# Output projection of a mixer on one core: three chunks swept and five resident, the resident ones loaded directly, scaling shared, LayerNorm in two fused passes, VectorE's order fixed token tile by token tile

## The chip, the cores and the metric

The kernel runs on one core of a Trainium2 chip. The core has five engines with their own instruction queues: TensorE (PE, with PEld for its weight loads), VectorE (DVE), ScalarE (ACT), GpSimd (POOL) and SyncE (SP), which here issues nearly all DMAs. The engines wait for each other through semaphores. The metric is the device time of one execution in microseconds (us), the median of several runs. The programs are built by a scheduler that puts the instructions of each engine into one fixed order, so what stands behind a waiting instruction on its engine waits with it.

## The reference, cut to what matters

One post-norm layer on 512 tokens of width 1024, in float32. The change touches the end of the first sub-layer and the beginning of the second, and a helper that the last projection shares.

```
def _token_mixer(...):
    ...
    merged = gates[:, :, 0] * y_a + gates[:, :, 1] * y_b + gates[:, :, 2] * y_c
    return merged @ w_o
...
def _conv_ffn(h, w_up, conv_w, conv_b, w_down):
    z = h @ w_up                      # 1024 -> 5632
    ...                               # causal convolution of width 3
    return (jax.nn.silu(gate) * val) @ w_down   # 2816 -> 1024
...
x = LayerNorm(ALPHA * x + gate_t * _token_mixer(...)) * gain + bias
h = LayerNorm(x) * (1 + scale_f) + shift_f
x = LayerNorm(ALPHA * x + gate_f * _conv_ffn(h, ...)) * gain + bias
```

`gate_t`, `scale_f` and the like are rows that depend on the condition `c` only.

## The kernel before, in words

Every float32 matrix product is made of three products of rounded parts: an operand `w` is split into a high part `wh` and a remainder `wl`, and `mm3` (L103 to L106) issues wl·xh, wh·xl, wh·xh into one accumulator. The splitting costs ScalarE a copy (high part) and VectorE a subtraction (low part).

Tokens come in four tiles of 128 (t = 0 to 3), widths in halves of 512 (n = 0, 1). Weights come in chunks of 128 rows.

**The merge and the projection.** `merge(2, m, ...)` makes eight tiles `mg` with GpSimd (L374) and splits them into `mgh` and `mgl` (L986, L987). `project_out` (L1018) then multiplies by the eight chunks of `wo`, into eight accumulators `pyo` (one for each t and n). A chunk is loaded and scaled by the gate row `gttb` on GpSimd, both halves (`scaled_chunk`, L998 to L1016, the multiplication at L1003), and split. The first two chunks are swept: `o`, `oh`, `ol` are 1024 wide and live in rings of two, and each chunk goes through all eight accumulators. The other six are resident: their split parts (`o2h`, `o2l` and so on) have buffers of their own, so that the program can run token tile by token tile. All raw chunks come through one ring of three buffers with the tag `raw` (L82), which the early chunks of the next weight share. The same function makes the down projection at the end, with 22 chunks (`d`, 18 swept and 4 resident).

**Behind each token tile.** `chain(t, acc)` is `after_mixer`. It does, for two halves each: `residual` (VectorE: x1 = ALPHA·xr + pyo, L1079, and statistics, L1082), `ln_finish` (VectorE aggregates, L129; GpSimd computes 1/sqrt(var), a multiply-add L120, a power L123 and a product L132), `affine` (ScalarE, L1086), `gain_bias` (half 0 on GpSimd, half 1 on VectorE, multiplication L1092 and addition L1093), `second_stats` (VectorE, L1106, and `ln_finish` again), `second_norm` (ScalarE writes `xr`, L1113). When two token tiles are done, `second_modulation(tp, jp)` transposes them on TensorE (`pth`, L1125), and ScalarE and VectorE write `h2T0h`, `h2T0l` to `h2T7h`, `h2T7l` (L1133 to L1145).

**The up projection.** Six early pieces of `wup` (m = 0 to 5, split in `early_split` and `early_low`, L1049 to L1067) are multiplied with the first two token tiles as soon as `h2T` has them (`pzu`, 256 columns, `up_early`), later with the other two; the remaining 38 pieces run with all 512 columns.

**The gate row.** `gt_t = ada_rows(0, 0, "gtt")` (L809) sums up a row: ScalarE splits, GpSimd subtracts (`adal`, L734), four `pgt` products on TensorE (L739), and VectorE adds a bias. It stands between the first merge and the pooling products (`pmx`).

The order comes from a scheduler, save for a few places pinned with `issue_after`: `behind_split` puts condition rows behind a weight split, and `after(...)` with `marks` holds some of the second token pair's work behind `second_modulation`.

Of the kernel before, what the change touches and what calls it, by code (L numbers as in the profile page):

```python
# [50 lines left out]
def trunk(ctx: ExitStack, tc: tile.TileContext, A, out):  # L51
# [73 lines left out]
    last = []  # L125

    def ln_finish(st):
        mv = sm.tile([P, 2], F32, name="mv", tag="mv")
        a = nc.vector.bn_aggr(out=mv, in_=st.rearrange("p a b -> p (a b)"))  # L129
# [2 lines left out]
        b = nc.gpsimd.tensor_scalar(  # L132
            out=rs[:, 1:2], in0=mv[:, 0:1], scalar1=rs[:, 0:1], scalar2=-1.0, op0=ALU.mult, op1=ALU.mult
        )
# [864 lines left out]
    def scaled_chunk(src, gt, name, dst=None):  # L999
        raw = load(src, D, name)  # L1000
        for n in range(2):
            c = slice(n * 512, (n + 1) * 512)
            nc.gpsimd.tensor_tensor(out=raw[:, c], in0=raw[:, c], in1=gt[n], op=ALU.mult)  # L1003
        if dst is None:
            hi = wp.tile([P, D], F32R, name=name + "h", tag="whi")
            lo = wp.tile([P, D], F32R, name=name + "l", tag="wlo")
            nc.scalar.copy(out=hi, in_=raw)  # L1007
            nc.vector.tensor_tensor(out=lo, in0=raw, in1=f(hi), op=ALU.subtract)  # L1008
            return [hi[:, :512], hi[:, 512:]], [lo[:, :512], lo[:, 512:]]
        his = [dst(f"{name}h{n}") for n in range(2)]  # L1010
        los = [dst(f"{name}l{n}") for n in range(2)]
        for n in range(2):
# [2 lines left out]
            nc.vector.tensor_tensor(out=los[n], in0=raw[:, c], in1=f(his[n]), op=ALU.subtract)
# [52 lines left out]

    def residual_in(t):
        xr[t] = [act_t(f"xr{t}{n}", F32) for n in range(2)]  # L1070
        for n in range(2):
# [3 lines left out]
        x1[t] = [m_t(f"x1_{t}{n}") for n in range(2)]
        st_o[t] = sm.tile([P, 2, 6], F32, name="sto", tag="sto")

    def residual(t, n):
        nc.vector.scalar_tensor_tensor(  # L1079
            out=x1[t][n], in0=xr[t][n], scalar=ALPHA, in1=py_o[t][n], op0=ALU.mult, op1=ALU.add  # L1080
        )
        nc.vector.bn_stats(out=st_o[t][:, n, :], in_=x1[t][n])  # L1082

    def affine(t):
        for n in range(2):
            nc.scalar.activation(  # L1086
                x1[t][n], x1[t][n], AF.Identity, bias=rs_o[t][:, 1:2], scale=rs_o[t][:, 0:1]
            )

    def gain_bias(t):  # L1090
        for n, eng in ((0, nc.gpsimd), (1, nc.vector)):
            eng.tensor_tensor(out=x1[t][n], in0=x1[t][n], in1=lntg[n], op=ALU.mult)  # L1092
            eng.tensor_tensor(out=x1[t][n], in0=x1[t][n], in1=lntb[n], op=ALU.add)  # L1093
# [320 lines left out]
```

## Time and profile before

| | us |
|---|---|
| time, median of three runs | 1004.75 (1003.79 to 1005.43) |
| the profiled execution, its own time | 1005.82 |
| its span in the profile | 1003.7 |
| TensorE busy | 965.4 (96%) |
| VectorE, ScalarE, GpSimd busy | 601.0, 386.6, 301.1 |

The granted TensorE clock was 0.987 over the span. The profiled execution took 1005.82, so 2.1 us lie outside its span, and it is 1.07 above the median of the three runs. TensorE is busy nearly everywhere, so the time is the sum of its matmuls and of the places where it waits; the views that show those places are the list of waits and the timeline.

### The profile page before, as it was taken

Reading aid. Unit: us, or ns where it says so; the run is one execution under the profiler, and the core shown is the slowest. Engines: PE = TensorE matmul, PEld = TensorE weight load, DVE = VectorE, ACT = ScalarE, POOL = GpSimd, SP = SyncE. Lnnn points to the kernel's source line nnn. Section 1 sums busy time; section 2 is a strip of 40 time slices with the busy share of each in tenths; the row PEclk is TensorE's granted clock in tenths of the full one; section 3 lists DMA queues with packets and bytes.
Section 4 is the critical chain, followed back from the end, with each engine's and each line's share of the span. In section 5 each row is a group of like instructions: output and inputs, shape, how many; then the busy total and the mean of one; then the engine's idle time right before and its main releaser. Section 6 shows DMA issues by size and latency. Waiting matters only on the chain.

```text
span 1003.7 us, 12194 instructions
## 1 busy us (share of the span) xinstructions
PE 965.4 (96%) x4530; PEld 801.5 (80%) x4530; DVE 601.0 (60%) x923; ACT 386.6 (39%) x656; POOL 301.1 (30%) x311
## 2 busy tenths in 40 slices
PE   4999999999999999999999997999999999999996
PEld 3888888878877888888888876998888888788885
DVE  6947655546666565666434477777656675532267
ACT  3555555442323322433232234554434444321221
POOL 3555110212350011200011755421111121566664
PEclk9999999999999999999999998999999999999998
DMA  9713111115444542363222263124333433342322
GB/s 336 267 39 93 48 51 51 57 63 189 148 131 148 191 136 97 105 220 126 75 93 89 92 225 118 42 84 128 125 121 110 126 126 106 91 140 89 101 84 84
DMA packets 45274, 119.18 MB, mean 119 GB/s; under 512 B 5280, under 2 KB 8736, under 8 KB 45216
## 3 DMA queue, kind: packets, MB, share of 16 engines
q1 hardware_dynamic: 44784, 118.25, 36.0%
q8 instruction: 35, 0.57, 0.2%
q10 hardware_dynamic: 432, 0.17, 0.1%
q14 instruction: 23, 0.19, 0.1%
HBM read 116.30 MB, written 2.10 MB: 118 GB/s over the span
## 4 chain that ended last, share of the span: by engine, by line
PE 77%; DVE 6%; DMA 6%; POOL 5%; issue 3%; ACT 2%; SPq 0%; DVEq 0%; POOLq 0%; ACTq 0%
PE pzu L104 7%; PE pzu L106 7%; PE pzu L105 7%; PE pg L105 4%; PE pg L104 4%; PE pg L106 4%; PE pyd L106 4%; PE pyd L105 4%; PE pyd L104 4%; PE py L104 3%; PE py L105 3%; PE py L106 3%; PE pu L105 3%; PE pu L106 3%; PE pu L104 3%
## 5 line engine op out<-in xcount | busy, mean ns | idle before, releaser
L1270 POOL TENSOR_TENSOR zc<-zc 128x512 f32<-128x512 f32 x22 | 32.7, 1484 | 179.1 <-ACT zc L1269 179.1
L1003 POOL TENSOR_TENSOR d<-d,gtfb 128x512 f32<-128x512 f32 x44 | 72.9, 1676 | 42.1 <-DMA d<-in_wdn 39.3
L374 POOL TENSOR_TENSOR mg<-mg,th 128x512 f32<-128x512 f32 x16 | 22.7, 1416 | 150.5 <-DVE th L371 150.5
L1255 DVE SCALAR_TENSOR_TENSOR zc<-pzu,cols,zc 128x511 f32<-128x511 f32 x44 | 32.8, 747 | 50.1 <-ACT zc L1252 49.9
L1252 ACT ACTIVATE zc<-pzu,cols 128x512 f32<-128x512 f32 x44 | 34.2, 779 | 71.2 <-PE pzu L106 71.2
L1008 DVE TENSOR_TENSOR dl<-d,dh 128x1024 fp32r<-128x1024 f32 x18 | 29.0, 1613 | 52.1 <-ACT dh L1007 52.1
L91 DVE TENSOR_TENSOR wgl<-wg,wgh 128x1024 fp32r<-128x1024 f32 x22 | 27.7, 1260 | 48.6 <-ACT wgh L90 47.4
L721 DVE SCALAR_TENSOR_TENSOR ada<-adar,cact,ada 128x512 f32<-128x512 f32 x56 | 54.6, 1015 | 0.1
L90 ACT CAST wbh<-wb 128x1024 fp32r<-128x1024 f32 x24 | 25.2, 1051 | 70.3 <-PE py L106 65.9
L91 DVE TENSOR_TENSOR wbl<-wb,wbh 128x1024 fp32r<-128x1024 f32 x24 | 38.3, 1595 | 18.4 <-ACT wbh L90 18.3
L91 DVE TENSOR_TENSOR wupl<-wup,wuph 128x1024 fp32r<-128x1024 f32 x38 | 46.9, 1234 | 0.0
L1007 ACT CAST dh<-d 128x1024 fp32r<-128x1024 f32 x18 | 18.9, 1050 | 60.7 <-PE pyd L106 60.6
L90 ACT CAST wuph<-wup 128x1024 fp32r<-128x1024 f32 x38 | 39.5, 1039 | 0.0
L91 DVE TENSOR_TENSOR wsgl<-wsg,wsgh 128x1024 fp32r<-128x1024 f32 x16 | 19.6, 1224 | 33.2 <-ACT wsgh L90 33.2
L354 ACT ACTIVATE th<-pg 128x512 f32<-128x512 f32 x22 | 13.1, 597 | 59.5 <-PE pg L106 59.5
L1259 DVE SCALAR_TENSOR_TENSOR zc<-pzu,cols,zc 128x510 f32<-128x510 f32 x44 | 32.7, 747 | 1.3
L90 ACT CAST wsgh<-wsg 128x1024 fp32r<-128x1024 f32 x16 | 16.8, 1050 | 42.8 <-PE pu L106 38.0
L1003 POOL TENSOR_TENSOR o<-o,gttb 128x512 f32<-128x512 f32 x16 | 26.4, 1677 | 19.6 <-DMA o<-in_wo 16.7
L254 DVE SCALAR_TENSOR_TENSOR acc<-ada,cact,acc 128x256 f32<-128x256 f32 x48 | 29.2, 671 | 0.0
L642 POOL TENSOR_SCALAR pe<-pe,mx 128x128 f32<-128x128 f32 (+3 forms) x32 | 16.8, 533 | 35.7 <-DVE mx L641 26.3
L90 ACT CAST wgh<-wg 128x1024 fp32r<-128x1024 f32 x22 | 23.1, 1051 | 10.1 <-PE pu L106 4.7
L776 POOL TENSOR_TENSOR asum<-apad 128x527 f32<-128x527 f32 x8 | 8.5, 1065 | 56.8 <-issue 25.8
(1375 smaller groups left out, 3182.9 us busy)
## 6 DMA issues: line engine op xcount, KB each, us to landing
wup<-in_wup SPq DMA_DIRECT2D x44, 512.0 KB, 3.5
adar<-in_ada SPq DMA_DIRECT2D x64, 256.0 KB, 3.9
wb<-in_wb SPq DMA_DIRECT2D x24, 512.0 KB, 3.5
wg<-in_wg SPq DMA_DIRECT2D x22, 512.0 KB, 3.6
d<-in_wdn SPq DMA_DIRECT2D x22, 512.0 KB, 3.5
ada<-in_ada SPq DMA_DIRECT2D x32, 256.0 KB, 5.0
wsg<-in_wsg SPq DMA_DIRECT2D x16, 512.0 KB, 3.6
wa<-in_wa SPq DMA_DIRECT2D x8, 512.0 KB, 3.6
```

Of the source, the lines that this page charges most:

```text
L90: nc.scalar.copy(out=hi[:, :n], in_=raw[:, :n])
L91: ins = nc.vector.tensor_tensor(out=lo[:, :n], in0=raw[:, :n], in1=f(hi[:, :n]), op=ALU.subtract)
L104: nc.tensor.matmul(o, wh, xl, start=start, stop=False)
L105: nc.tensor.matmul(o, wl, xh, start=False, stop=False)
L106: nc.tensor.matmul(o, wh, xh, start=False, stop=stop)
L254: ins = nc.vector.scalar_tensor_tensor(out=acc[i], in0=src, scalar=cact[:, k : k + 1], in1=acc[i], op0=ALU.mult, op1=ALU.add,)
L721: nc.vector.scalar_tensor_tensor(out=acc[n], in0=src, scalar=cact[:, k : k + 1], in1=acc[n], op0=ALU.mult, op1=ALU.add,)
L1003: nc.gpsimd.tensor_tensor(out=raw[:, c], in0=raw[:, c], in1=gt[n], op=ALU.mult)
L1252: nc.scalar.activation(t, pz, AF.Identity, bias=cols[:, cc + 3 : cc + 4], scale=cols[:, cc + 2 : cc + 3])
L1255: nc.vector.scalar_tensor_tensor(out=t[:, 1:512], in0=pz[:, 0:511], scalar=cols[:, cc + 1 : cc + 2], in1=t[:, 1:512], op0=ALU.mult, op1=AL ...
L1259: nc.vector.scalar_tensor_tensor(out=t[:, 2:512], in0=pz[:, 0:510], scalar=cols[:, cc : cc + 1], in1=t[:, 2:512], op0=ALU.mult, op1=ALU.add,)
L1270: nc.gpsimd.tensor_tensor(out=val, in0=val, in1=gate, op=ALU.mult)
```

## The change

Five things are done.

1. `ada_rows(0, 0, "gtt")` moves from behind the first merge to the middle of the gating mixer's v halves.
2. The projection has three swept chunks and five resident ones. A resident chunk, in this projection and in the down projection, is loaded as two halves straight into buffers of the `act` pool (`o3w`, `d18w` and so on), no longer through the ring `raw`.
3. In the mixer's projection half 0 of a chunk is scaled on GpSimd and half 1 on VectorE; in the down projection both stay on GpSimd.
4. The first LayerNorm is made of two fused VectorE passes: `centre`, (x − mean)·gain, and `scale_again`, x·rs + bias, with the statistics of the second norm behind it. ScalarE's `affine` and the multiplications and additions of `gain_bias` go. `x` is loaded before the projection into the buffers that held `mg`, and becomes x1 in place.
5. VectorE's order around the token tiles is fixed with `in_turn`: the splits of `wup` 1 to 4 first, then tile 0 complete, tile 1 complete, then tiles 2 and 3 with the modulations between.

```
-    gt_t = ada_rows(0, 0, "gtt")
...
     v0 = uv_half(2, "v", lambda q: behind_split(ada_piece, 1, q))
+    gt_t = ada_rows(0, 0, "gtt")
...
     def scaled_chunk(src, gt, name, dst=None):
-        raw = load(src, D, name)
-        for n in range(2):
-            c = slice(n * 512, (n + 1) * 512)
-            nc.gpsimd.tensor_tensor(out=raw[:, c], in0=raw[:, c], in1=gt[n], op=ALU.mult)
+        if dst is None:
+            raw = load(src, D, name)
+            parts = [raw[:, :512], raw[:, 512:]]
+        else:
+            his = [dst(f"{name}h{n}") for n in range(2)]
+            los = [dst(f"{name}l{n}") for n in range(2)]
+            parts = [act_t(f"{name}w{n}", F32) for n in range(2)]
+            for n in range(2):
+                nc.sync.dma_start(out=parts[n], in_=src[:, n * 512 : (n + 1) * 512])
+        for n, eng in ((0, nc.gpsimd), (1, nc.vector if name[0] == "o" else nc.gpsimd)):
+            eng.tensor_tensor(out=parts[n], in0=parts[n], in1=gt[n], op=ALU.mult)
...
+    def in_turn(work, *args):
+        with ExitStack() as order:
+            for ins in vector_order:
+                order.enter_context(tc.issue_after(ins))
+            vector_order[:] = [work(*args).ins]
...
+    def residual(t):
+        ...
+            nc.vector.scalar_tensor_tensor(
+                out=x1[t][n], in0=x1[t][n], scalar=ALPHA, in1=py_o[t][n], op0=ALU.mult, op1=ALU.add
+            )
+            nc.vector.bn_stats(out=st[:, n, :], in_=x1[t][n])
+        ...
+    def centre(t):
+        for n in range(2):
+            ins = nc.vector.scalar_tensor_tensor(
+                out=x1[t][n], in0=x1[t][n], scalar=mv_o[t][:, 0:1], in1=lntg[n],
+                op0=ALU.subtract, op1=ALU.mult,
+            )
+        return ins
+
+    def scale_again(t):
+        ...
+            nc.vector.scalar_tensor_tensor(
+                out=x1[t][n], in0=x1[t][n], scalar=rs_o[t][:, 0:1], in1=lntb[n],
+                op0=ALU.mult, op1=ALU.add,
+            )
+            nc.vector.bn_stats(out=st[:, n, :], in_=x1[t][n])
+        rs_o[t] = ln_finish(st)
...
-    def affine(t):
-        for n in range(2):
             nc.scalar.activation(
-                x1[t][n], x1[t][n], AF.Identity, bias=rs_o[t][:, 1:2], scale=rs_o[t][:, 0:1]
-            )
-
-    def gain_bias(t):
-        for n, eng in ((0, nc.gpsimd), (1, nc.vector)):
-            eng.tensor_tensor(out=x1[t][n], in0=x1[t][n], in1=lntg[n], op=ALU.mult)
-            eng.tensor_tensor(out=x1[t][n], in0=x1[t][n], in1=lntb[n], op=ALU.add)
...
     def after_mixer(t, py):
         py_o[t] = py
+        in_turn(residual, t)
         if t == 2:
+            in_turn(second_modulation, 0, 0)
+        in_turn(centre, t)
+        if t == 2:
+            in_turn(second_modulation, 0, 1)
+        in_turn(scale_again, t)
+        second_norm(t)
+        if t == 2:
+            in_turn(second_modulation, 0, 2)
+            in_turn(second_modulation, 0, 3)
+            early_split(5)
+            early_low(5, nc.gpsimd)
...
-    project_out(lambda k: A["wo"][k], KT, 6, mg_hi, mg_lo, gt_t, act_t, after_mixer, "o")
+    project_out(
+        lambda k: A["wo"][k], KT, 5, mg_hi, mg_lo, gt_t, act_t, after_mixer, "o", before_tokens
+    )
```

How the built order moves is seen at three places. The first is TensorE where token tile 0 gets its last products of the projection. `pyo_5095` and `pyo_5096` are the two halves of tile 0 before, `pyo_5097` and `pyo_5098` those of tile 1; these rows are the 104th to 114th of the projection's 192 matmuls. Before:

```order
L104 MATMUL pyo_5095<-o7l0_5233,mgh7_5067 128x512
L105 MATMUL pyo_5095<-o7h0_5231,mgl7_5068 128x512
L106 MATMUL pyo_5095<-o7h0_5231,mgh7_5067 128x512
L104 MATMUL pyo_5097<-o7l0_5233,mgh7_5067 128x512
L105 MATMUL pyo_5097<-o7h0_5231,mgl7_5068 128x512
L106 MATMUL pyo_5097<-o7h0_5231,mgh7_5067 128x512
L104 MATMUL pyo_5098<-o5l1_5210,mgh5_4999 128x512
L105 MATMUL pyo_5098<-o5h1_5208,mgl5_5000 128x512
L104 MATMUL pyo_5096<-o7l1_5234,mgh7_5067 128x512
L105 MATMUL pyo_5096<-o7h1_5232,mgl7_5068 128x512
L106 MATMUL pyo_5096<-o7h1_5232,mgh7_5067 128x512
```

Now tile 0 has `pyo_5121` and `pyo_5122`, tile 1 `pyo_5123` and `pyo_5124`, and `pyo_5128` is the last half of tile 3; the rows are the 166th to 177th of the 192:

```order
L104 MATMUL pyo_5128<-o6l1_5270,mgh6_5036 128x512
L104 MATMUL pyo_5121<-o7l0_5283,mgh7_5067 128x512
L105 MATMUL pyo_5121<-o7h0_5281,mgl7_5068 128x512
L106 MATMUL pyo_5121<-o7h0_5281,mgh7_5067 128x512
L104 MATMUL pyo_5122<-o7l1_5284,mgh7_5067 128x512
L105 MATMUL pyo_5122<-o7h1_5282,mgl7_5068 128x512
L106 MATMUL pyo_5122<-o7h1_5282,mgh7_5067 128x512
L104 MATMUL pyo_5123<-o7l0_5283,mgh7_5067 128x512
L105 MATMUL pyo_5123<-o7h0_5281,mgl7_5068 128x512
L106 MATMUL pyo_5123<-o7h0_5281,mgh7_5067 128x512
L104 MATMUL pyo_5124<-o7l1_5284,mgh7_5067 128x512
L105 MATMUL pyo_5124<-o7h1_5282,mgl7_5068 128x512
```

Tile 0's two halves were complete after matmul 106 and 114 of 192, and are now after 169 and 172; tile 1's moved from 109 and 121 to 175 and 178. TensorE now runs the resident chunks chunk by chunk.

The second place is VectorE behind the projection's last split. Before, the work of the first two token tiles (`x1_0`, `x1_1`) starts between splits of `wup`:

```order
L1065 TENSOR_TENSOR upl01_5280<-wup_5275,uph01_5278 128x512
L1015 TENSOR_TENSOR o7l1_5234<-o7_5227,o7h1_5232 128x512
L1079 SCALAR_TENSOR_TENSOR x1_00_5289<-xr00_5285,pyo_5095 128x512
L1082 BN_STATS sto_5291<-x1_00_5289 128x6
L1079 SCALAR_TENSOR_TENSOR x1_01_5290<-xr01_5286,pyo_5096 128x512
L1079 SCALAR_TENSOR_TENSOR x1_10_5306<-xr10_5302,pyo_5097 128x512
L1065 TENSOR_TENSOR wupl_5325<-wup_5322,wuph_5324 128x512
L1082 BN_STATS sto_5291<-x1_01_5290 128x6
```

Now the splits of `wup` 1 to 4 stand ahead, and behind them tile 0 as a whole (shown without buffer numbers of `pyo`, `mv` and `rs`; `x_00` and `x_01` are tile 0's halves):

```order
L1089 SCALAR_TENSOR_TENSOR x_00_5105<-x_00_5105,pyo 128x512
L1089 SCALAR_TENSOR_TENSOR x_01_5106<-x_01_5106,pyo 128x512
L1092 BN_STATS sto<-x_00_5105 128x6
L1092 BN_STATS sto<-x_01_5106 128x6
L1094 BN_AGGR mv<-sto 128x2
L1101 SCALAR_TENSOR_TENSOR x_00_5105<-x_00_5105,mv,lntg_5071 128x512
L1101 SCALAR_TENSOR_TENSOR x_01_5106<-x_01_5106,mv,lntg_5073 128x512
L1110 SCALAR_TENSOR_TENSOR x_00_5105<-x_00_5105,rs,lntb_5075 128x512
L1110 SCALAR_TENSOR_TENSOR x_01_5106<-x_01_5106,rs,lntb_5077 128x512
L1114 BN_STATS st<-x_00_5105 128x6
L1114 BN_STATS st<-x_01_5106 128x6
L129 BN_AGGR mv<-st 128x2
```

Tile 1's first instruction stood three places behind tile 0's first; it now follows the last of these twelve, and tile 1's own twelve come before anything of tile 2.

The third place is ScalarE in the down projection, where `dh` is the high part of a swept chunk (18 in all), and `d18h` to `d21h` those of the resident ones. Before, they come at the end, behind fifteen more swept chunks:

```order
L1007 CAST dh<-d 128x1024 x15
L1014 CAST d18h_8125<-d_8121 128x512
L1014 CAST d18h_8126<-d_8121 128x512
L1007 CAST dh<-d 128x1024
L1014 CAST d19h_8137<-d_8133 128x512
L1014 CAST d19h_8138<-d_8133 128x512
```

Now they stand between the fourth and the eighth swept chunk:

```order
L1017 CAST d18h_8115<-d18w_8119 128x512
L1012 CAST dh<-d 128x1024
L1017 CAST d18h_8116<-d18w_8120 128x512
L1017 CAST d19h_8129<-d19w_8133 128x512
L1017 CAST d19h_8130<-d19w_8134 128x512
L1012 CAST dh<-d 128x1024
L1017 CAST d20h_8143<-d20w_8147 128x512
L1017 CAST d20h_8144<-d20w_8148 128x512
L1017 CAST d21h_8157<-d21w_8161 128x512
L1012 CAST dh<-d 128x1024
```

GpSimd scales them in the same order, so a swept chunk's `dh` now waits behind resident ones on both engines.

More of the change, by code (lines that the diff above doesn't have):

```diff
@@ L1030, in project_out @@
         ws = {k: scaled_chunk(src(k), gt, f"{name}{k}", dst) for k in range(nk - resident, nk)}
+        if hook:
+            hook()
         for t in range(TT):
@@ new lines, in centre @@
+    def centre(t):
+        for n in range(2):
+            ins = nc.vector.scalar_tensor_tensor(
+                out=x1[t][n], in0=x1[t][n], scalar=mv_o[t][:, 0:1], in1=lntg[n],
+                op0=ALU.subtract, op1=ALU.mult,
+            )
+        return ins
+    def scale_again(t):
+        st = sm.tile([P, 2, 6], F32, name="st", tag="st")
+        for n in range(2):
+            nc.vector.scalar_tensor_tensor(
[4 more added lines that the diff above has]
+        rs_o[t] = ln_finish(st)
+        return aggregated[0]
@@ L1070, in residual_in, with second_norm @@
+    def second_norm(t):
         xr[t] = [act_t(f"xr{t}{n}", F32) for n in range(2)]
         for n in range(2):
-            nc.sync.dma_start(
-                out=xr[t][n], in_=A["x"][t * P : (t + 1) * P, n * 512 : (n + 1) * 512]
-            )
[L1075 to L1080, printed above, removed]
-        )
-        nc.vector.bn_stats(out=st_o[t][:, n, :], in_=x1[t][n])
@@ L1103, in second_stats @@
-    def second_stats(t):
-        st = sm.tile([P, 2, 6], F32, name="st", tag="st")
-        for n in (1, 0):
-            nc.vector.bn_stats(out=st[:, n, :], in_=x1[t][n])
-        rs = ln_finish(st)
-        marks[t] = list(last)
-        return rs
-    def second_norm(t, rs):
-        for n in range(2):
-            a = nc.scalar.activation(
-                xr[t][n], x1[t][n], AF.Identity, bias=rs[:, 1:2], scale=rs[:, 0:1]
-            )
-        marks[t].append(a.ins)
+            nc.scalar.activation(
+                xr[t][n], x1[t][n], AF.Identity, bias=rs_o[t][:, 1:2], scale=rs_o[t][:, 0:1]
+            )
@@ L1210, in trunk @@
+    early_split(0)
+    early_low(0, nc.vector)
+    for t in range(TT):
+        x1[t] = [m_t(f"x1_{t}{n}") for n in range(2)]
+        for n in range(2):
+            nc.sync.dma_start(
+                out=x1[t][n], in_=A["x"][t * P : (t + 1) * P, n * 512 : (n + 1) * 512]
+            )
+    project_out(
+        lambda k: A["wo"][k], KT, 5, mg_hi, mg_lo, gt_t, act_t, after_mixer, "o", before_tokens
+    )
     pzs = {}
@@ L1243, in trunk @@
             else:
-                with after(3) if m < NE + 2 else ExitStack():
-                    uh, ul = wsplit(A["wup"][m], D, "wup")
+                uh, ul = wsplit(A["wup"][m], D, "wup")
                 pz = ps("pzu")
```

118 lines of the change are left out of this document (33 added, 85 removed).

## The prediction, made before the changed kernel was run

> **What bounds the kernel now.** Read first is the page's line of busy times, then the list of TensorE's waits (engine, line waited for: us in total, times, longest), then TensorE's timeline (start, us, instruction, and in brackets the idle time before it and what ended it).
>
> ```profile
> PE 965.4 (96%) x4530; PEld 801.5 (80%) x4530; DVE 601.0 (60%) x923; ACT 386.6 (39%) x656; POOL 301.1 (30%) x311
> ...
> PE pth L1125 <- ACT xr L1113: 5.7, 2, 4.6
> ...
> PE pgt L739 <- POOL adal L734: 1.2, 2, 0.7
> PE pyd L104 <- DVE dl L1008: 1.0, 2, 0.8
> ...
> PE pyo L104 <- DVE o5l L1015: 0.7, 1, 0.7
> ```
>
> TensorE is busy 96% of the span, so a change pays only where TensorE waits. The waits near the change are these four: behind the projection (`pth`), at the gate row (`pgt`), in the projection (`pyo`), and a small one in the down projection (`pyd`).
>
> ```profile
> 569.46 0.40 PE L104 MATMUL pyo<-ol,mgh 128*128 128x512 f32 x1
> ...
> 588.77 0.50 PE L104 MATMUL pyo<-o5l,mgh 128*128 128x512 f32 x1 [0.65 <-DVE o5l L1015]
> ...
> 615.66 0.39 PE L106 MATMUL pyo<-o7h,mgh 128*128 128x512 f32 x1
> 620.60 1.39 PE L1125 MATMUL pth<-ident,xr 128*128 128x128 f32 x4 [4.56 <-ACT xr L1113]
> 623.10 2.82 PE L1125 MATMUL pth<-ident,xr 128*128 128x128 f32 x12 [1.11 <-ACT xr L1113]
> 625.58 0.58 PE L104 MATMUL pzu<-h2T0l,uph 128*128 128x256 f32 x1
> ...
> 631.05 0.39 PE L104 MATMUL pzu<-h2T2l,uph 128*128 128x256 f32 x1 [0.83 <-DVE h2T2l L1145]
> ...
> 664.78 0.28 PE L106 MATMUL pzu<-h2T7h,uph 128*128 128x256 f32 x1
> 664.90 0.63 PE L104 MATMUL pzu<-h2T0l,wuph 128*128 128x512 f32 x2
> ```
>
> I call E the start of the projection's last matmul, 615.66. The up projection starts at E + 9.9, and its first matmul with all 512 columns, behind which nothing of this stage is late any more, at E + 49.2. Everything that the change does to LayerNorm must show in that second number. The windows (length, busy time and count of PE, PEld, DVE, ACT, POOL, then the granted clock) show the clock in the halt, and the pace of undisturbed matmuls (here PE alone):
>
> ```profile
> 616.00:620.50 4.50, 0.04 (x1) 0.00 (x0) 4.47 (x9) 0.76 (x2) 3.59 (x6) 0.81 0.00 0
> 620.50:629.00 8.50, 7.27 (x32) 6.43 (x33) 4.69 (x8) 7.23 (x14) 5.41 (x11) 0.50 0.00 0
> ...
> 873.60:995.20 121.60, 121.42 (x528) 1.00 0.31 100
> ```
>
> 528 matmuls of 512 columns in 121.6 are 0.230 each; one of 256 columns takes 0.12 (664.78 to 664.90).
>
> **The gate row: −1.8.**
>
> ```profile
> 300.24 0.40 PE L106 MATMUL py<-o7h,wbh 128*128 128x512 f32 x1
> 301.37 0.50 PE L739 MATMUL pgt<-adal,onesr 128*128 128x512 f32 x1 [0.73 <-POOL adal L734]
> ...
> 303.18 0.39 PE L104 MATMUL pmx<-po0l,wpoolh 128*128 128x512 f32 x1
> ```
>
> From 300.24 to 303.18 five steps take 2.94, where five steps of 0.230 are 1.15: 1.8 are waits for GpSimd's `adal`. In its new place the row was summed long before, and the four `pgt` stand amid gating matmuls. It could gain nothing, if `pmx` then waits for the pooling sums, and not more than 1.8; I take 1.8, as no `pmx` wait stands in the list.
>
> **The projection itself: −2.3.** Its 191 steps last 615.66 − 569.46 = 46.2, and at 0.230 they would last 43.9. The 2.3 are waits for low parts from `o5l` on (the list holds the two largest). GpSimd explains them:
>
> ```profile
> L1003 POOL TENSOR_TENSOR o<-o,gttb 128x512 f32<-128x512 f32 x16 | 26.4, 1677 | 19.6 <-DMA o<-in_wo 16.7 <-DVE mgl L987 2.9
> ```
>
> It scaled 16 halves at 1.677, and stood idle 16.7 for their loads, since all chunks pass a ring of three. Now five chunks have buffers of their own, and GpSimd scales half as much. TensorE also needs them later: chunk 3 after 72 matmuls (16.6), each next one 5.5 further. Bounds: 2.3 gained, or, if `o3` and `o4` are each as late as `o5` was, 2.3 gained and as much lost again. I take the gain. VectorE gets eight multiplications more, hidden behind the 5.5 per chunk.
>
> **LayerNorm: +4.7.** This is the term that decides. Tile 0 was complete 78 matmuls ahead of the end (114 of 192), so most of two LayerNorms lay beside the projection. Now it is complete after matmul 169 and 172: the 169th starts 23 × 0.230 = 5.3 ahead of E and ends 0.39 later, so VectorE can begin at E − 4.9. What it then does in a row is priced by these (in the second piece: line, names, count | busy, mean ns):
>
> ```profile
> 607.82 0.69 DVE L1082 BATCH_NORM_STATS2 sto<-x 128x6 f32<-128x512 f32 x1
> 608.42 0.67 DVE L1079 SCALAR_TENSOR_TENSOR x<-xr,pyo 128x512 f32<-128x512 f32 x1
> 609.01 0.20 DVE L129 BATCH_NORM_AGGREGATE mv<-sto 128x2 f32<-128x12 f32 x1
> ```
>
> ```profile
> L1295 DVE SCALAR_TENSOR_TENSOR out<-out,mv,lnfg 128x512 f32<-128x512 f32 x8 | 5.7, 749 | 0.1
> ```
>
> Starts lie 0.60 apart for a statistic or a residual, 0.08 less than its duration; the fused form, which the last LayerNorm already uses, takes 0.749, so a pace of 0.67. A tile is 2 residuals and 4 statistics at 0.60, 4 fused passes at 0.67, 2 aggregations at 0.2: 6.7, and some 0.3 where an instruction needs the one ahead of it: 7.0. Two tiles, one behind the other, end at E + 9.1. The power between the two passes lies beside `centre` (two passes, 1.4) but for the 0.2 within that 0.3:
>
> ```profile
> 606.54 0.20 DVE L129 BATCH_NORM_AGGREGATE mv<-sto 128x2 f32<-128x12 f32 x1
> ...
> 606.85 0.51 POOL L120 TENSOR_SCALAR pw<-mv 128x1 f32<-128x1 f32 x1 [6.30 <-DVE mv L129]
> 607.44 0.88 POOL L123 TENSOR_TENSOR rs<-pw,neghalf 128x1 f32<-128x1 f32 x1
> 608.42 0.27 POOL L132 TENSOR_SCALAR rs<-mv,rs 128x1 f32<-128x1 f32 x1
> ...
> 608.72 1.52 ACT L1086 ACTIVATE x<-x,rs 128x512 f32<-128x512 f32 x2 [1.75 <-POOL rs L132]
> ```
>
> From the aggregate's end to ScalarE are 2.0 here, and 1.8 where the power isn't slowed; I take 1.8: `xr` of tile 1 starts at E + 10.9.
>
> ```profile
> 622.24 1.52 ACT L1113 ACTIVATE xr<-x,rs 128x512 f32<-128x512 f32 x2 [0.98 <-POOL rs L132]
> ...
> 625.09 0.43 DVE L1145 TENSOR_TENSOR h2T0l<-h2f,h2T0h 128x256 fp32r<-128x256 f32 x1 [3.25 <-ACT h2T0h L1142]
> 625.55 0.54 DVE L1137 TENSOR_SCALAR h2T1h<-pth,scfc,shfc 128x256 fp32r<-128x256 f32 x1
> 626.12 0.42 DVE L1145 TENSOR_TENSOR h2T1l<-h2f,h2T1h 128x256 fp32r<-128x256 f32 x1
> ```
>
> From there to the first `pzu` were 3.3 (622.24 to 625.58), so the up projection starts at E + 14.2, 4.3 later than before.
>
> Then the second token pair is late. VectorE reaches `h2T0l` at 10.9 + 2.85 = E + 13.75. It still owes tile 2's fused passes and second statistics (4.3), four pairs of modulation writes (1.3 each by the last three rows: 5.2) and all of tile 3 (7.0): E + 30.3. `upl5` on GpSimd now falls beside tile 3's `centre`, which has a price:
>
> ```profile
> 615.81 1.17 DVE L1092 TENSOR_TENSOR x<-x,lntg 128x512 f32<-128x512 f32 x1 [1.00 <-ACT x L1086]
> ...
> 617.62 0.68 DVE L1079 SCALAR_TENSOR_TENSOR x<-xr,pyo 128x512 f32<-128x512 f32 x1
> ```
>
> ```profile
> 617.11 1.72 POOL L1093 TENSOR_TENSOR x<-x,lntb 128x512 f32<-128x512 f32 x1
> ```
>
> Beside a GpSimd operation the one with both inputs in SBUF took 1.17 instead of 0.68, while the residual, which reads an accumulator, kept 0.68. One such slowing is 0.5: E + 30.8, and with 1.8 and 3.3 the second half can start at E + 35.9. TensorE is done with the first half at 14.2 + 144 × 0.12 + 1.5 (16 matmuls at half clock) + 0.5 = E + 33.5, so it waits 2.4. Then 144 matmuls and some transposes, 18.0: E + 53.9 against E + 49.2, or **+4.7**. Bounds: +2.3 if the second wait vanishes, +8.4 with the first rival below.
>
> **The down projection: +0.3.**
>
> ```profile
> L1003 POOL TENSOR_TENSOR d<-d,gtfb 128x512 f32<-128x512 f32 x29 | 49.5, 1725 | 29.9 <-DMA d<-in_wdn 29.8
> ```
>
> ```profile
> 882.69 2.32 DVE L1008 TENSOR_TENSOR dl<-d,dh 128x1024 fp32r<-128x1024 f32 x1
> ```
>
> GpSimd was idle 29.9 of this stage (880 to 960), so the eight resident halves fit, but now among chunks 4 to 7. From d4's start (about 881) to the end of `d21`'s first half are 13 scalings at 1.725: 903.4, then 0.6 on ScalarE. Only then may `dh` of chunk 6 begin, which must begin by about 903.7: chunk 6 is due at 873.6 + 6 × 5.53 + the 1.0 of `pyd`, less 1.05 for `dh`, 2.32 for `dl` and hand-overs. It is 0.3 late; bounds 0 (fewer slowed scalings) and 2 (more).
>
> **The sum.** −1.8 − 2.3 + 4.7 + 0.3 = +0.9. On the profiled execution's 1005.82 that is 1006.7; the median of the runs is 1.07 lower, so I forecast 1004.75 + 0.9, rounded **1005.6**. The removed ScalarE and GpSimd passes gain nothing by themselves, as both engines wait in that stage.
>
> **The rivals.**
>
> *A second halt at half clock (slower).* If tile 3 is later still (its `pw` stands behind both `upl5` on GpSimd, and both `centre` passes take 1.17), TensorE waits 4.4 instead of 2.4. A halt of 4.56 brought the clock to 0.50 above, one of 0.83 did not. Half clock then costs another 1.5 to 1.7: 1005.6 + 2.0 + 1.7 = 1009.3. It decides from a halt somewhere between the 2.4 of my sum and the 4.56 of the row; against it, my sum stays below. The Trainium skill (TensorE: Matmul & The Clock Gate, What's actually happening) says that an idle window of some 3.4 us halves the clock and a busy one restores it. By that rule 2.4 leaves the sum as it is and 4.4 gives 1009.3; the trace's 0.81 and 0.50 agree.
>
> *The direct loads don't come earlier (it doesn't do what it says).* SP's queue puts the last `x` loads and a `wup` load ahead of `o3`, and each waits for a buffer. Then the 2.3 stay: 1007.9. For it: GpSimd's 16.7 were all waits for loads. Against it: 16.6 of matmuls cover chunk 3.
>
> *The down projection jams.* The upper bound of 2 instead of 0.3: 1007.3.
>
> *The chain is short (faster).* VectorE at 0.60 everywhere saves 1.5 on two tiles, TensorE's second wait vanishes, so LayerNorm costs 2.3, and the 1.0 of `pyd` goes: −1.8 − 2.3 + 2.3 − 1.0 = −2.8, or 1002.0. Against it: the fused form took 0.749 in the trace, and the second wait has tile 3's whole work before it.
>
> **How the numbers follow.** My sum 0.47, with its own range of 1003.8 to 1007.4; the second halt 0.16; the late loads 0.10; the jam 0.10; the short chain 0.17. A measurement of this kernel tells about 0.2%, or 2.0 us, from no change, so the limits are 1002.7 and 1006.8. Faster is the short chain, 0.16. Within are 0.43 of the sum and 0.06 of the others: 0.49. Slower is the rest, 0.35. The range from 1001.8 to 1009.4 leaves out half of the short chain and half of the second halt.
>
> **What would show it.** `pgt` leaves the list of waits (right) or `pmx` enters it (wrong). The projection lasts 43.9 from first to last matmul; a `pyo` wait for `o3l` or `o4l` means late loads. The first `pzu` stands 14.2 behind E and the first 512-column `pzu` 53.9; below 52 the short chain holds, above 56 the second halt, which the clock there would show below 1.0. The `pyd` waits stay at 1.0 to 1.5. The forecast is wrong if VectorE waits within the two tiles' chain, or TensorE gets tile 0 earlier than its order says.

## The result, and the profile after

The change makes the kernel a little slower: 1010.44 us (median of four runs, 1008.59 to 1013.57) against 1004.27 (four runs, 1002.36 to 1005.43), a ratio of 1.0066 with a 95% interval of 1.0047 to 1.0085. The forecast was 1005.6 with a range of 1001.8 to 1009.4. The profiled execution took 1008.59, the fastest of its four; its span is 1006.8.

First the busy times, then TensorE's waits (us in total, times, longest):

```profile
PE 960.7 (95%) x4530; PEld 798.6 (79%) x4530; DVE 608.1 (60%) x940; ACT 380.7 (38%) x647; POOL 275.8 (27%) x289
```

```profile
PE pth L1132 <- ACT xr L1121: 11.1, 4, 5.4
PE pyd L104 <- DVE dl L1013: 3.5, 3, 2.3
...
PE pzu L104 <- DVE h2T0l L1152: 1.2, 1, 1.2
PE pyo L104 <- DVE o3l L1018: 0.7, 1, 0.7
```

The gate row's waits are gone. Behind the projection 11.1 stand instead of 5.7, in the down projection 3.5 instead of 1.0, and a wait for `h2T0l` is new. To see what each is worth, the program is cut into stages at TensorE's own rows. For before, these are the rows of the first and the last cuts:

```profile
222.91 0.39 PE L104 MATMUL py<-o0l,wbh 128*128 128x512 f32 x1
...
873.62 0.51 PE L104 MATMUL pyd<-dl,f0h 128*128 128x512 f32 x1 [0.85 <-DVE dl L1008]
...
994.81 0.40 PE L106 MATMUL pyd<-d21h,f21h 128*128 128x512 f32 x1
```

The same cuts of after (TensorE's timeline: start, us, instruction, idle before it):

```profile
220.56 0.39 PE L104 MATMUL py<-o0l,wbh 128*128 128x512 f32 x1
...
565.30 0.39 PE L104 MATMUL pyo<-ol,mgh 128*128 128x512 f32 x1
...
609.80 0.39 PE L106 MATMUL pyo<-o7h,mgh 128*128 128x512 f32 x1
614.76 0.44 PE L1132 MATMUL pth<-ident,xr 128*128 128x128 f32 x2 [4.57 <-ACT xr L1121]
...
621.58 2.82 PE L1132 MATMUL pth<-ident,xr 128*128 128x128 f32 x12 [5.42 <-ACT xr L1121]
624.05 0.58 PE L104 MATMUL pzu<-h2T0l,uph 128*128 128x256 f32 x1
...
664.96 0.40 PE L104 MATMUL pzu<-h2T0l,wuph 128*128 128x512 f32 x1
...
873.87 0.50 PE L104 MATMUL pyd<-dl,f0h 128*128 128x512 f32 x1 [0.79 <-DVE dl L1013]
...
910.09 0.50 PE L104 MATMUL pyd<-dl,f6h 128*128 128x512 f32 x1 [2.34 <-DVE dl L1013]
...
997.88 0.40 PE L106 MATMUL pyd<-d21h,f21h 128*128 128x512 f32 x1
```

The differences of these starts, for all kernels of this study (E is the start of the projection's last matmul):

| kernel | first `py` to first `pyo` | projection | E to first `pzu` | E to first 512-column `pzu` | down projection | first `py` to last `pyd` |
|---|---|---|---|---|---|---|
| before | 346.6 | 46.2 | 9.9 | 49.2 | 121.2 | 771.9 |
| after | 344.7 | 44.5 | 14.3 | 55.2 | 124.0 | 777.3 |
| d_old | 344.7 | 44.2 | 14.8 | 54.1 | 121.9 | 773.7 |
| gate_alone | 344.8 | 44.5 | 9.2 | 48.6 | 121.4 | 767.8 |
| gate_back | 348.6 | 43.8 | 14.8 | 55.7 | 124.4 | 781.3 |
| late_before | 348.6 | 43.7 | 19.2 | 58.6 | 121.7 | 781.2 |
| pairs1 | 344.8 | 43.5 | 11.5 | 50.9 | 125.5 | 773.4 |
| early5 | 344.8 | 44.5 | 14.8 | 53.3 | 124.3 | 775.7 |
| o_ring | 344.7 | 53.3 | 2.3 | 43.1 | 124.1 | 773.8 |
| unfused | 344.7 | 44.5 | 16.7 | 62.4 | 124.1 | 784.5 |
| free | 344.7 | 49.6 | 21.5 | 59.5 | 124.0 | 786.5 |
| pool_scale | 344.7 | 47.9 | 15.8 | 55.3 | 124.1 | 780.9 |
| best1 | 344.7 | 44.7 | 12.8 | 51.2 | 121.3 | 770.9 |
| best3 | 344.8 | 44.6 | 11.2 | 49.4 | 121.8 | 769.2 |

The part between the first 512-column `pzu` and the down projection takes 208.5 to 209.0 in all of them. What lies ahead of the first `py` scatters between 220.4 and 223.5 from one profiled execution to the next, and is left out; that is why the two spans differ by only 3.1. The last column differs from before's by 5.4 for after, and by no more than 2.1 from what the medians show in any experiment, so it is the scale on which parts are weighed here.

For the change: −1.8 ahead of the projection (the gate row), −1.7 in it, **+5.9** from E to the first full `pzu`, +0.2 in the up projection, **+2.8** in the down projection.

**The second halt.** The first `pzu` is 4.3 later than before, as its late start has it. The other 1.6 of the 5.9 arise when the second token pair comes (TensorE's timeline; then windows: length, PE busy and count, granted clock, DMA share, GB/s):

```profile
643.35 0.87 PE L1132 MATMUL pth<-ident,xr 128*128 128x128 f32 x6 [0.83 <-ACT xr L1121]
645.47 0.39 PE L104 MATMUL pzu<-h2T0l,uph 128*128 128x256 f32 x1 [1.24 <-DVE h2T0l L1152]
...
646.20 0.42 PE L105 MATMUL pzu<-h2T0h,upl 128*128 128x256 f32 x1
646.42 0.41 PE L106 MATMUL pzu<-h2T0h,uph 128*128 128x256 f32 x1
```

```profile
644.00:647.00 3.00, 1.76 (x11) 0.81 0.00 0
647.00:650.00 3.00, 3.00 (x19) 0.63 0.00 0
```

TensorE waited 0.83 and 1.24, with a few small transposes between them. Then the starts lie 0.21 apart instead of 0.12, until about 649.2: the two windows lack 0.19 × 3 + 0.37 × 3 = 1.7 of full clock, so some 3.4 us ran at half. Sixteen matmuls at 0.09 more are the 1.5.

**The down projection.** GpSimd scales what SP has loaded (GpSimd's timeline; SP's queue; SP's waits from 880 to 886; GpSimd's window: length, its busy time and count, clock, DMA share, GB/s; and ScalarE's row behind it):

```profile
885.62 1.30 POOL L1008 TENSOR_TENSOR d18w<-d18w,gtfb 128x512 f32<-128x512 f32 x1 [1.27 <-DMA d18w<-in_wdn]
889.20 2.55 POOL L1008 TENSOR_TENSOR d<-d,gtfb 128x512 f32<-128x512 f32 x2 [2.29 <-DMA d<-in_wdn]
...
903.84 1.74 POOL L1008 TENSOR_TENSOR d21w<-d21w,gtfb 128x512 f32<-128x512 f32 x1
```

```profile
880.03 0.43 SPq L1006 DMA_DIRECT2D d18w<-in_wdn  x1
885.49 0.33 SPq L83 DMA_DIRECT2D d<-in_wdn  x1
885.92 0.38 SPq L1006 DMA_DIRECT2D d18w<-in_wdn  x1
```

```profile
SPq L83 <- DVE dl L1013: 5.0, 1, 5.0
```

```profile
881.30:905.60 24.30, 20.74 (x15) 1.00 0.58 197
```

```profile
906.14 1.05 ACT L1012 CAST dh<-d 128x1024 fp32r<-128x1024 f32 x1
```

The resident halves have buffers of their own, but swept chunks stand between them, whose loads still go through the ring, and SP issues both in one queue: it waited 5.0 for `dl`, which frees a ring buffer, and issued nothing from 880.03 to 885.49. GpSimd stood idle for 1.27 until the first half of `d18w` had landed, issued at 880.03, and for 2.29 until the swept chunk issued at 885.49 had; every later resident half stands behind that chunk in GpSimd's order. The last resident scaling ahead of chunk 6's `dh` ended at 905.6, ScalarE began that `dh` at 906.14, and TensorE waited 2.34.

### The profile page after: what moved, and what is told of

The parts are those of the page before. It is cut to its first block, busy times and chain, and to the rows that moved or that the text cites. A ratio compares the mean times of both kernels' runs of the same rounds, so it can differ in the third digit from the quotient of the medians.

```text
span 1006.8 us, 12164 instructions
## 1 busy us (share of the span) xinstructions
PE 960.7 (95%) x4530; PEld 798.6 (79%) x4530; DVE 608.1 (60%) x940; ACT 380.7 (38%) x647; POOL 275.8 (27%) x289
## 4 chain that ended last, share of the span: by engine, by line
PE 80%; POOL 5%; DVE 4%; DMA 4%; issue 4%; ACT 2%; SPq 0%; DVEq 0%; POOLq 0%
PE pzu L105 7%; PE pzu L106 7%; PE pzu L104 7%; PE py L104 4%; PE py L105 4%; PE py L106 4%; PE pg L105 4%; PE pg L104 4%; PE pg L106 4%; PE pyd L104 3%; PE pyd L106 3%; PE pyd L105 3%; PE pu L104 3%; PE pu L106 3%; PE pu L105 3%
## 5 line engine op out<-in xcount | busy, mean ns | idle before, releaser
L373 POOL TENSOR_TENSOR mg<-mg,th 128x512 f32<-128x512 f32 x16 | 26.5, 1654 | 162.7 <-DVE th L370 162.7
L1008 POOL TENSOR_TENSOR d<-d,gtfb 128x512 f32<-128x512 f32 x36 | 57.6, 1618 | 28.0 <-DMA d<-in_wdn 22.9
L90 ACT CAST wsgh<-wsg 128x1024 fp32r<-128x1024 f32 x16 | 16.8, 1049 | 43.8 <-PE pu L106 43.3
L91 DVE TENSOR_TENSOR wal<-wa,wah 128x1024 fp32r<-128x1024 f32 x8 | 10.3, 1287 | 23.4 <-ACT wah L90 23.4
L120 POOL TENSOR_SCALAR pw<-mv 128x1 f32<-128x1 f32 x12 | 5.5, 454 | 67.1 <-DVE mv L1271 29.2
```

Source lines behind the costliest of these rows:

```text
L90: nc.scalar.copy(out=hi[:, :n], in_=raw[:, :n])
L91: ins = nc.vector.tensor_tensor(out=lo[:, :n], in0=raw[:, :n], in1=f(hi[:, :n]), op=ALU.subtract)
L1008: eng.tensor_tensor(out=parts[n], in0=parts[n], in1=gt[n], op=ALU.mult)
```

## The experiments

The theory: the change loses by two side effects. With direct loads the scheduler runs the resident chunks chunk by chunk, so token tile 0 is late; and the resident loads and scalings jam the down projection. The rivals: the loss comes from the fused passes, the fixed order or the shared scaling themselves; from half clock alone; or the gate row and the direct loads don't bring what they seem to.

### d_old: the down projection's loads as before

```
+            if name[0] == "o":
                 parts = [act_t(f"{name}w{n}", F32) for n in range(2)]
...
+            else:
+                raw = load(src, D, name)
+                parts = [raw[:, :512], raw[:, 512:]]
```

> The changed kernel with its down projection as before (the four resident chunks of it through the ring of three again). Theory A, the resident scalings amid chunks 4 to 7 make GpSimd late and ScalarE with it: from the first to the last pyd 124.0 becomes about 121.2 as before, the pyd wait of 2.3 goes, and the time falls by 2.8 against the changed kernel (ratio to before about 1.003). Rival B, it is the transfers of the directly loaded halves or something in the up projection that makes chunk 6 late: pyd stays at 123 to 124 and a wait of about 2 stays.

Measured: 1005.26 (ten runs), 1.0010 of before (0.9997 to 1.0023), 5.2 below after, where 2.8 were expected. Its waits in the down projection are

```profile
PE pyd L104 <- DVE dl L1017: 1.5, 2, 0.8
```

and the stage lasts 121.9. The jam is confirmed. Of the 3.6 less in the last column 2.2 lie there; 1.0 more come from the second halt, where the two waits are 0.50 and 1.24 and this execution shows no half clock:

```profile
643.00:650.00 7.00, 5.26 (x43) 1.00 0.00 0
```

### gate_alone and gate_back: the gate row

gate_alone is before with nothing but the row moved; gate_back is after with the row at its old place.

```
-    gt_t = ada_rows(0, 0, "gtt")
...
     v0 = uv_half(2, "v", lambda q: behind_split(ada_piece, 1, q))
+    gt_t = ada_rows(0, 0, "gtt")
```

> The kernel before with the gate row alone moved. Theory A: pgt's two waits go and nothing takes their place: from the last py ahead of pmx to the projection's first matmul 1.8 less, time 1.8 less (ratio 0.998). Rival: pmx waits for the pooling sums instead, or the row is late for the projection's first scaling, and the time stays.

> The changed kernel with the gate row back in its old place. It tells what shortened the projection from 46.2 to 44.5, since the gate row moved alone gave 44.5 too. Theory A1, direct loads do it by themselves: the projection stays at 44 to 45 here, pgt's two waits return, and the time is 1.8 above the changed kernel. Theory A2, it is the moment at which the loads of wo fall, which the gate row shifted: the projection goes back to 46, and the time is 3 to 4 above the changed kernel.

gate_alone took **1000.63** (999.88 to 1001.85, four runs), 0.9962 of before (0.9948 to 0.9977): 3.6 instead of the 1.8 expected, the fastest kernel of the study. In the table 4.1 are gained: 1.8 by the row, 0.7 from E to the first full `pzu`, and 1.7 in the projection, although its built order is before's: it has no `pyo` wait. VectorE's row of `o2l` in before, then in gate_alone, and behind each SP's row of the next loads:

```profile
578.48 3.49 DVE L1015 TENSOR_TENSOR o2l<-o,o2h 128x512 fp32r<-128x512 f32 x2
```

```profile
582.04 2.69 SPq L83 DMA_DIRECT2D o<-in_wo  x3
```

```profile
574.70 2.39 DVE L1014 TENSOR_TENSOR o2l<-o,o2h 128x512 fp32r<-128x512 f32 x2
```

```profile
577.16 3.79 SPq L83 DMA_DIRECT2D o<-in_wo  x3
```

Chunk 5's load waits for `o2`'s ring buffer, that is for the end of `o2l`, which took 1.1 less here. All of it lies in the first half, 1.78 in before and 0.68 here. In before GpSimd began to scale the next chunk at 578.37, 0.11 ahead of that half; in gate_alone at 574.72, 0.02 behind it. So a tenth of a microsecond seems to decide; no run tests that by itself, nor whether it falls this way in every execution.

gate_back took 1013.33, 1.0097 (1.0073 to 1.0121), some 3 above after, with intervals that overlap. The stretch ahead of the projection is 3.9 longer than after's, twice the 1.8, because here the row's two short waits of TensorE (1.8 in the list) brought half clock; late_before, below, shows the rows. Its projection takes 43.8: the direct loads do end the `pyo` waits. But so does gate_alone without them. The change's 1.7 in the projection thus can't be credited to the direct loads: with the gate row moved, both ways take 44.5.

### late_before, pairs1 and o_ring: TensorE's order over the resident chunks

late_before is before with the resident chunks pinned chunk by chunk (tile 0 complete after 174 of 192 matmuls); pairs1 is after with chunk 3 pinned for all tiles, then chunks 4 to 7 for tiles 0 and 1, then for 2 and 3 (tile 0 after 138); o_ring is after with the mixer's resident chunks through the ring, where the scheduler itself puts tile 0 at 102.

```
# pairs1; late_before has one loop over k, t, n in the same manner
+        def pinned(t, n, k):
+            with ExitStack() as order:
+                for ins in prev:
+                    order.enter_context(tc.issue_after(ins))
+                prev[:] = [step(t, n, k, ws[k]).ins]
...
+        for pair in ((0, 1), (2, 3)):
+            for k in range(r0 + 1, nk - 1):
+                for t in pair:
+                    for n in range(2):
+                        pinned(t, n, k)
...
# o_ring
+            if name[0] == "o":
+                raw = load(src, D, name)
+                parts = [raw[:, :512], raw[:, 512:]]
```

> The kernel before, with nothing changed but TensorE's order in the projection, pinned chunk by chunk as in the changed kernel, so that tile 0 is complete after 171 and 174 of 192 instead of 106 and 114. Theory A, the late start is the loss, and the fused passes in a fixed order are a gain that makes up for part of it: the first pzu comes 18 to 21 behind the projection's end (9.9 before, 14.2 changed), the first 512-column pzu at 56 to 60 (49.2, 55.2), the time 7 to 10 above before. Rival B, the loss is the fused passes on VectorE: with the old passes the late start costs little, the first pzu stays below 14 and the time within 4 of before.

> The changed kernel with TensorE's order pinned: chunk 3 through all tiles, then chunks 4 to 7 for tiles 0 and 1, then for tiles 2 and 3, so that tile 0 is complete after matmul 135 to 138 of 192 instead of 169 to 172. Theory A, the late start of tile 0 is what LayerNorm's loss comes from: VectorE's chain begins some 7.8 earlier against the projection's end, the first pzu comes 7 to 9 behind it instead of 14.2, the first 512-column pzu at 47 to 50 instead of 55.2, and the time falls by 5 to 7 against the changed kernel. Rival B, the fused passes make VectorE itself the bound wherever tile 0 starts: first pzu stays above 12 and the time within 2. Rival C, chunks 5 to 7 aren't there yet in this order: pyo waits of 3 or more and a projection of 48 or longer eat it up.

> The changed kernel with the mixer's five resident chunks through the ring of three again (the down projection stays direct). In its built order tile 0 is complete after 96 and 102 of 192 matmuls, so it tells whether the direct loads brought the late start. Theory A, they did: the projection itself lasts 4 to 6 longer (pyo waits for the ring come back, 49 to 50 from first to last), but LayerNorm's chain lies beside it, the first pzu comes 3 to 5 behind the projection's end instead of 14.2, and the time is 4 to 6 below the changed kernel. Rival, the waits in the projection eat it up: the first 512-column pzu is no earlier against the projection's first matmul (99.7 in the changed kernel), time within 2 of it.

late_before: 1012.88, 1.0085 (1.0068 to 1.0101). A late tile 0 alone, with the old passes, moves the first `pzu` to E + 19.2 (after: 14.3), and the wait list has

```profile
PE pth L1139 <- ACT xr L1127: 15.0, 2, 13.1
```

So the late start is the loss, and the fused passes with their fixed order win part of it back. Not all of the 8.6 above before is the late start, though: in the table 9.4 lie behind E, the projection is 2.5 shorter, and 2.0 lie ahead of it, where the order wasn't changed. There, at the gate row, this execution shows half clock (TensorE's timeline and windows):

```profile
299.12 0.50 PE L739 MATMUL pgt<-adal,onesr 128*128 128x512 f32 x1 [0.74 <-POOL adal L734]
...
300.89 0.57 PE L739 MATMUL pgt<-adal,onesr 128*128 128x512 f32 x1 [1.05 <-POOL adal L734]
```

```profile
300.00:303.00 3.00, 2.10 (x6) 0.70 0.17 11
303.00:306.00 3.00, 3.00 (x11) 0.74 0.46 164
```

pairs1: 1006.32, 1.0022 (1.0007 to 1.0038), 4.1 below after. The first `pzu` came at E + 11.5, not at the 7 to 9 I had expected: VectorE's chain began with `wup` 4's low part, which waited for its load.

```profile
600.13 1.29 DVE L1100 TENSOR_TENSOR upl<-wup,uph 128x512 fp32r<-128x512 f32 x2 [1.82 <-ACT uph L1094]
```

Its down projection is 1.5 longer than after's with the same waits, since here half clock followed the wait ahead of chunk 6 (2.38; in after 2.34, with the clock at 1.00):

```profile
906.00:909.00 3.00, 3.00 (x9) 0.50 0.54 172
```

o_ring: 1005.56, 1.0017 (1.0001 to 1.0033). Projection and LayerNorm, from the first `pyo` to the first full `pzu`, take 96.4 together, against 99.7 in after. The loads through the ring keep tile 0 early, at the price of a projection of 53.3 (I had expected 49 to 50). Two things make it long. TensorE waits for low parts, 4.2 in all, and the first transposes of LayerNorm, which elsewhere lie behind E, stand ahead of the projection's last matmuls, with a wait of 1.90 and half clock from 613 to 617:

```profile
PE pyo L104 <- DVE ol L1017: 1.9, 2, 1.3
...
PE pyo L104 <- DVE o5l L1022: 1.8, 1, 1.8
```

```profile
613.08 0.44 PE L1136 MATMUL pth<-ident,xr 128*128 128x128 f32 x2 [1.90 <-ACT xr L1125]
```

Before takes 95.4 and gate_alone 93.1, so this way doesn't pay either.

### early5: `wup` 5 split ahead of the token tiles

```
         for m in range(1, 5):
             early_split(m)
             in_turn(early_low, m, nc.vector)
+        early_split(5)
+        early_low(5, nc.gpsimd)
...
-            early_split(5)
-            early_low(5, nc.gpsimd)
```

> The changed kernel with the split of wup 5 ahead of the token tiles, so that GpSimd's two subtractions no longer lie beside tile 3's centre nor ahead of its power. Theory A, the second halt is tile 3's chain and halves the clock for one window: centre of tile 3 falls from 2.39 to 1.4, its xr starts about 2 earlier, the waits before the second half fall from 2.1 to under 0.5, no half clock at 645 to 650, first 512-column pzu at 51 to 52 behind the projection's end instead of 55.2, time 3 less. Rival B, the clock falls in that stage for another reason (a window of transposes): the halt shrinks but the matmuls behind it still run at 0.21 for 3.4, and only about 1.5 are won.

Measured: 1007.51, 1.0035 (1.0024 to 1.0047), 2.9 below after. Tile 3's `centre` in after, then in early5, is

```profile
635.49 2.39 DVE L1101 SCALAR_TENSOR_TENSOR x<-x,mv,lntg 128x512 f32<-128x512 f32 x2
```

```profile
636.61 1.41 DVE L1101 SCALAR_TENSOR_TENSOR x<-x,mv,lntg 128x512 f32<-128x512 f32 x2
```

so GpSimd's `upl5` had cost 1.0 there. The wait of 0.83 is gone, but the wait for `h2T0l` stayed at 1.2, where under 0.5 was expected; this execution shows no half clock (1.00 from 643 to 647), and the first full `pzu` comes at E + 53.3 (51 to 52 expected). That the missing wait took the half clock away isn't shown. pairs1 has the same two waits as after, and its clock stayed (TensorE's timeline and a window):

```profile
640.12 0.87 PE L1159 MATMUL pth<-ident,xr 128*128 128x128 f32 x6 [0.84 <-ACT xr L1148]
642.23 0.39 PE L104 MATMUL pzu<-h2T0l,uph 128*128 128x256 f32 x1 [1.24 <-DVE h2T0l L1179]
```

```profile
644.00:647.00 3.00, 3.00 (x29) 1.00 0.00 0
```

So did pool_scale's (0.85 and 1.24), while in gate_back (0.85 and 1.24) and o_ring (0.84 and 1.24) half clock followed, as in after.

### unfused, free and pool_scale: the parts taken back one by one

unfused has the passes of before (ScalarE's `affine`, then GpSimd and VectorE one half each) at the change's place, with tiles 0 and 1 interleaved on VectorE; free drops VectorE's fixed order; pool_scale scales both halves on GpSimd.

```
# unfused
-            nc.vector.scalar_tensor_tensor(out=x1[t][n], in0=x1[t][n], scalar=mv_o[t][:, 0:1], in1=lntg[n], ...)
+            nc.scalar.activation(x1[t][n], x1[t][n], AF.Identity, bias=rs_o[t][:, 1:2], scale=rs_o[t][:, 0:1])
+        nc.gpsimd.tensor_tensor(out=x1[t][0], in0=x1[t][0], in1=lntg[0], op=ALU.mult)
...
# free
-            for ins in vector_order:
-                order.enter_context(tc.issue_after(ins))
# pool_scale
-        for n, eng in ((0, nc.gpsimd), (1, nc.vector if name[0] == "o" else nc.gpsimd)):
+        for n, eng in ((0, nc.gpsimd), (1, nc.gpsimd)):
```

> The changed kernel with the old passes of the first LayerNorm (ScalarE's affine, multiplication and addition of the halves on GpSimd and VectorE), the first two tiles interleaved on VectorE so that it needn't wait. Theory A, fusing is a gain where tile 0 starts late: the chain now runs through three engines, the first pzu comes at 16 to 18 behind the projection's end instead of 14.2, the first 512-column pzu at 58 to 61, time 3 to 6 above the changed kernel. Rival B, VectorE's added work is the loss: first pzu at 12 or less and the time 2 or more below the changed kernel.

> The changed kernel without VectorE's fixed order (no in_turn edges). Theory A, the fixed order is a gain: left to itself the scheduler mixes the tiles and completes tile 0 after 171 and 183, the first pzu comes at 20 to 23 behind the projection's end instead of 14.2, time 7 to 10 above the changed kernel. Rival B, it is the fixed order that costs: first pzu below 13, time 2 or more below the changed kernel.

> The changed kernel with both halves of the mixer's chunks scaled on GpSimd. Theory A, sharing gains a little: the halves come later, pyo waits of 1 in all more, tile 0 complete after 171 and 179, first pzu 15 to 16 behind the projection's end, time 1 to 3 above the changed kernel. Rival, VectorE gains the eight multiplications back and the time falls by 1 or more.

All three medians lie above after's, so none of the three parts looks like the loss. Only free's interval is clear of after's (1.0047 to 1.0085):

| | median | ratio to before | what it shows |
|---|---|---|---|
| unfused | 1014.73 | 1.0100 (1.0083 to 1.0117) | first full `pzu` 7.2 later than after; half clock lasts twice as long (waits of 2.81 and 1.13) |
| free (two runs) | 1019.08 | 1.0148 (1.0128 to 1.0169) | projection 5.1 longer (it waits 5.2 for `o3l`, `o4l` and `o5l`), first `pzu` at E + 21.5 |
| pool_scale (two runs) | 1013.39 | 1.0092 (1.0073 to 1.0110) | projection 3.4 longer, about half of it half clock from 585 to 589 |

In pool_scale GpSimd's chunk 3 is late, as the row of its wait says:

```profile
PE pyo L104 <- DVE o3l L1018: 2.3, 1, 2.3
```

### best1 and best3: the losses repaired

Both are after with d_old's loads and pairs1's order, and with the low parts of `wup` 4 and 5 on GpSimd: in best1 ahead of the tiles, in best3 behind the second norm of tiles 0 and 1.

```
# best3
         in_turn(scale_again, t)
         second_norm(t)
+        if t < 2:
+            early_split(4 + t)
+            with tc.issue_after(negated[0].ins):
+                early_low(4 + t, nc.gpsimd)
```

> All that the runs so far found put together on the changed kernel: the down projection as before (2.5 to 3), TensorE's order with tiles 0 and 1 ahead (tile 0 complete after 135 and 138), and the splits of wup 4 and 5 on GpSimd ahead of the token tiles, so that VectorE's chain begins about 3 earlier than in that order alone. Theory A: first pzu at 8.5 to 10 behind the projection's end (11.5 with the order alone), first 512-column pzu at 47 to 49, pyd 121 to 122, time 5 below before (ratio 0.995). Rival: GpSimd's four subtractions beside the fused passes slow VectorE by as much as they take from it, first pzu at 11 or later, time within 2 of before.

> The last mixture once more, with GpSimd's subtractions for wup 4 and 5 pinned behind tile 0's and tile 1's second statistics, so that they no longer stand ahead of tile 0's power (which cost 3.4 in the last one). Theory A: VectorE's chain for two tiles begins 10 to 11 ahead of the projection's end and takes 14.3, first pzu at 8.5 to 10 behind it, first 512-column pzu at 47.5 to 49, time 999 to 1001 (ratio 0.995 to 0.997). Rival: the late loads of wup 4 and 5 hold up the first half, waits of 2 or more ahead of pzu of pieces 4 and 5, time 1002 or more.

best1: 1003.35, 0.9991 (0.9979 to 1.0003), with the first `pzu` at E + 12.8: the rival's outcome, though the delay lies elsewhere. The subtractions stood ahead of tile 0's power on GpSimd, and VectorE waited for it (GpSimd's timeline, then VectorE's):

```profile
603.94 4.74 POOL L1104 TENSOR_TENSOR upl<-wup,uph 128x512 fp32r<-128x512 f32 x3 [11.35 <-DVE sto L1123]
```

```profile
610.90 1.41 DVE L1141 SCALAR_TENSOR_TENSOR x<-x,rs,lntb 128x512 f32<-128x512 f32 x2 [3.40 <-POOL rs L123]
```

best3: 1001.94 (eleven runs), 0.9979 (0.9970 to 0.9988). It beats before and after, though it missed the expected 999 to 1001, and its first `pzu` at E + 11.2 the expected 8.5 to 10. Against gate_alone it is 1.3 slower, with intervals that overlap: the repaired change brings nothing that can be measured beyond its gate row.

## Why the prediction was wrong

- **The gate row, −1.8:** right, measured −1.8. That its two waits can also bring half clock (gate_back: 3.9) was not foreseen.
- **The projection, −2.3:** measured −1.7, with one wait left, 0.7 for `o3l`: GpSimd's `o3w` waited for its load, as the second rival had it. The reason given holds only in part: the direct loads do end the other waits (gate_back), but gate_alone ends them without.
- **LayerNorm, +4.7:** measured +5.9. The working was right up to the second halt: the first `pzu` at E + 14.3 (forecast 14.2), the second half's start at 645.47, that is E + 35.7 (forecast 35.9). Luck had a part in the first: VectorE's chain for two tiles ended at E + 9.6, not 9.1, and 1.3 passed from there to ScalarE, not 1.8. The step that failed is "144 matmuls and some transposes, 18.0": they took 19.5, at half clock for their first part. The first rival had that mechanism, but put its point between halts of 2.4 and 4.56; here 2.07 of waits, in two pieces, were enough, and in pairs1 and pool_scale they were not. So the 1.5 was not a sure cost but a chance, which the sum put at nothing. The Trainium skill (TensorE: Matmul & The Clock Gate, What's actually happening) has the clock halved after an idle window of some 3.4 us and says that the window runs freely. The 3.4 us of half clock agree with that length, and equal waits with unequal outcomes fit a window that runs freely; no run here shows where the window stood.
- **The down projection, +0.3 with bounds 0 to 2:** measured +2.8, above its own bound, and the largest error. The step that failed is the time at which GpSimd is done with `d21`'s first half: it counted thirteen scalings without a gap from 881 and got 903.4. GpSimd was busy 20.7 of the 24.3 that they took, less than the 22.4 assumed, but idle for 1.27 and 2.29 between them, so they ended at 905.6. I had counted the ring's waits for loads as room that the resident halves would fill; but swept chunks stand between them in GpSimd's order, and their loads still waited for the ring. The third rival, the jam, had the direction, with a bound of 2.
- **The sum, +0.9:** 5.4 in the trace, 6.2 in the medians. Of the 4.5 missing 2.5 are the down projection, 1.2 LayerNorm, 0.6 the projection and 0.2 the up projection. Two of the rivals came together, the jam and the half clock; each had been priced alone, so the range didn't reach them both.

Shown by experiment: the jam (d_old), the loss by a late tile 0 (late_before, pairs1), and that VectorE's fixed order is a gain at its place (free). Fusion and shared scaling look like gains (unfused, pool_scale), but their intervals overlap after's. Only read from rows: that the ring's waits make GpSimd's gaps in the jam, and that the half clock in the second halt costs 1.5. It remains open what decides whether half clock follows a short wait, and how much of gate_alone's 3.6 is the row itself and how much the chance that `o2l` ended earlier.

## What to carry to other kernels

Giving some loads buffers of their own frees them only as far as the queue that issues them and the engine that prepares them are free: look for what stands ahead of each on both, above all for loads that still wait for a ring. Where a scheduler sets the order, look in the built order for when the first piece that others wait for is complete, since a change of loads alone can move it to the end. Test the smallest part of a change alone, here one moved line, before crediting the rest.
